# First modulation weights in tiles of 256 columns, first value products in halves of 256 features, router weights read later

## The chip, the cores and the metric

The kernel runs on one core of one Trainium2 chip. The metric is the device time of one execution in microseconds, given as the median of several runs. The profile comes from one more execution of the same program, recorded by the hardware profiler; its engines are named TensorE (PE, and PEld for its weight loads), VectorE (DVE), ScalarE (ACT), GpSimd (POOL) and SyncE (SP).

## The reference

Two layers of a diffusion backbone work on 256 latent tokens `x` and 256 context tokens `ctx` of 1024 features, all in float32. Only the start of layer 0 matters here:

```python
mod = jax.nn.silu(c) @ ada_w[layer] + ada_b[layer]
mod_c = jax.nn.silu(c_ctx) @ ada_w[layer] + ada_b[layer]
sh1, sc1, g1, sh2, sc2, g2 = [m[:, None, :] for m in jnp.split(mod, 6, axis=-1)]
...
xm = modulate(rmsnorm(h, norm_g[layer, 0]), sh1, sc1)      # x * (1 + sc1) + sh1
cm = modulate(rmsnorm(hc, norm_g[layer, 0]), sh1c, sc1c)
...
pl = xm @ w_in          # w_in: 1024 x 2560 = Fourier 256, q 768, k 768, v 768
pc = cm @ w_in
a_lat = fourier_mix(pl[..., :FNET_WIDTH])
```

After it come neighbourhood attention, an output projection, and a mixture of 16 experts whose router (`router_w`, `router_b`) picks two of them for a token. Layer 1 has retention with four decay matrices in place of the attention.

## The kernel before, in words

**Products in three parts.** A float32 product is done as three products of rounded float32: each operand is split into a high part (a rounded copy) and a low part (the rest). `mm3` (L318 to L320) issues high times high, low times high and high times low. For weights, `whi` is a copy on ScalarE (L176) and `wlo` a subtraction on VectorE or GpSimd (L178), both over 128x1024, so one tile of 1 MB has two of each.

**Weights.** All weights come in tiles of 1 MB on SyncE's queue, one after another in the order of the program, into a ring of four buffers called `raw` (L157). A load is issued when its buffer has been read for the last time; whatever stands behind it in the queue waits too. The first tiles are those of `ada_w`: 4 blocks of 128 rows by 512 columns, two tiles for a chunk of 512 of the 6144 modulation values. `ada_mm` (L259) loads a small bias `adab` (and for a scale the gain `adag`), multiplies the two columns of conditioning `cT` by the two tiles (L275), adds the bias on VectorE (L283, L285), turns the chunk by a TensorE transpose `ada_tp` (L289) and copies it to `modcol` (L290). Chunks 0 and 1 are the shift SH1, chunks 2 and 3 the scale SC1.

**The start of mixer0** (L354). `norm_t(t)` normalizes a block of 128 tokens (squares on ScalarE L218, a root on VectorE, the scaling `hn` L379), and sixteen transposes `nT` (L383) bring x's two blocks to features by tokens, copied by ScalarE into `mix` (L385). `modulate` (L388) takes a block of 128 features: scale and shift on VectorE (L397) or ScalarE (L395), the high part `xhi` on ScalarE (L399) and the low part `xlo` on VectorE (L400). The order is: x normalized, chunks 0 and 2, the first four blocks of x modulated, the first value weight tile split (one of its low parts on GpSimd), ctx loaded and normalized, its first four blocks modulated, chunks 1 and 3, and the last four blocks of both.

**Value products.** `v_ps` holds four PSUM tiles for the four blocks of tokens (two of x, two of ctx). The products over the first four feature blocks (kh 0) come first, for each token block t in turn, then those over the last four (kh 1), first for 512 columns of the values (n 0), then for the last 256 of them and the 256 Fourier columns (n 1), which ScalarE copies to `at` (L459).

**Decays and the Fourier part.** `decay_setup` makes four tables of decays (`d4`, one buffer) with eight exponentials each on ScalarE (L657, L660), masks and sums on VectorE (L661, L662), and a store of 512 KB from GpSimd's queue, `dmat` (L663). The exponentials of the next table that write into the buffer wait for the landing of the store before. Its inputs are read on ScalarE's queue (L621 the decay rates, L635 the distances `base`). The Fourier part multiplies `at` by a table (L465), copies the result to `ft` on ScalarE (L467), once for each of two halves b, and multiplies again (L472, L473). Then the query and key products `qk_ps` begin.

**The order of work.** Each engine and each queue executes its own list in order. A scheduler makes the lists of TensorE, ScalarE, VectorE and GpSimd from the program; `issue_after` adds a wish for one instruction to stand behind another. SyncE's list follows the program.

Of the kernel before, what the change touches and what calls it, by code (L numbers as in the profile page):

```python
# [7 lines left out]
F32 = mybir.dt.float32  # L8
# [4 lines left out]
ALU = mybir.AluOpType  # L13
# [8 lines left out]
SH1, SC1, G1, SH2, SC2, G2 = range(6)  # L22
C_ID, C_W4, C_PIDX, C_SEL, C_P = 0, 128, 132, 133, 149
C_U, C_IOTA = C_P, C_P + 128
# [53 lines left out]
def weight_tiles():  # L78
    t = {}
# [3 lines left out]
    t["ada_w"] = [((l,), 4 * i, 4, 512 * c, 512) for l in range(2) for c in range(12) for i in range(2)]  # L83
# [27 lines left out]
class Net:  # L111
# [110 lines left out]
    def prologue(self):  # L222
        nc, A = self.nc, self.A
# [13 lines left out]
        with self.tc.tile_pool(name="prop", bufs=1, space=PSUM, reuse_waits="tile") as p:  # L237
            tp = p.tile([128, 16], F32, name="ptp")
# [5 lines left out]
        nc.gpsimd.dma_start(self.rw, A["router_w"].rearrange("(k p) e -> p k e", p=128))  # L244
        self.rb = self.const.tile([128, 16], F32, name="rb")
        nc.gpsimd.dma_start(self.rb, A["router_b"].partition_broadcast(128))
        nc.gpsimd.tensor_scalar(self.rb, self.rb, 0.5, None, ALU.add)
# [4 lines left out]
        self.rbm = [self.const.tile([128, 16], F32, name=f"rbm{i}") for i in range(2)]  # L252

# [103 lines left out]
    def mixer0(self):  # L357
# [3 lines left out]
        with ExitStack() as es0:  # L361
# [5 lines left out]
            with ExitStack() as es:  # L367
# [5 lines left out]
                with ExitStack() as ea:  # L373
# [14 lines left out]
                    def modulate(k0, segs):  # L388
                        col = self.modcol[:, 0]
                        for k in range(k0, k0 + 4):  # L390
# [15 lines left out]
                    self.ada_chunk(0, 0, aps, psp)  # L406
                    self.ada_chunk(0, 2, aps, psp)
                    modulate(0, (0,))
                    self.prefetch_split([key(0, 4, 1792, 512)], 1)
                    nc.sync.dma_start(h[:, 2:4, :], A["ctx"].rearrange("(t p) d -> p t d", p=128))  # L410
                    norm_t(2)
                    norm_t(3)
# [7 lines left out]
                with ExitStack() as ea:  # L420
# [4 lines left out]
                    with tc.issue_after(ia.ins):  # L425
                        nc.scalar.dma_start(dft, A["cst"][:, C_BD:])
                        nc.scalar.dma_start(ui, A["cst"][:, C_U:C_U + 256])
# [8 lines left out]
                    for n in range(2):  # L436
# [5 lines left out]
                        for kh in range(2):  # L442
                            for t in range(4):
                                tk = slice(128 * t, 128 * t + 128)
                                with tc.issue_after(last.ins) if n + kh == 0 and t > 1 else ExitStack():
                                    for k in range(4 * kh, 4 * kh + 4):
                                        self.mm3(pss[t], (xhi[:, k, tk], xlo[:, k, tk]), self.wk(ws[kh], k % 4),
                                                 k == 0, k == 7)
                            if n:
                                self.ada_step(aps, psp)  # L450
# [1266 lines left out]
```

## Time and profile before

| | us |
|---|---|
| median of three runs (lowest, highest) | 1288.08 (1285.81, 1289.31) |
| the profiled execution's own time | 1290.84 |
| its span, from the first to the last instruction | 1289.0 |
| TensorE busy in the span | 1203.7 (93%) |
| VectorE busy | 941.8 (73%) |
| ScalarE busy | 755.6 (59%) |
| GpSimd busy | 124.5 (10%) |

A row of a timeline has the start, the busy time, the engine, the line, the operation, what is written from what, and the count of instructions in that row; the bracket tells how long the engine had been idle before it and what ended the idleness. A row of windows has the stretch and its length, then for each engine the busy time and the count, then the granted clock of TensorE as a share of its full 2.4 GHz, the mean busy share of the 16 DMA engines, and GB/s.

### The profile page before, as it was taken

What the parts mean: (1) busy time and instruction counts of PE and PEld (TensorE: products, weight loads), DVE (VectorE), ACT (ScalarE), POOL (GpSimd) and SP (SyncE); (2) the same over time, 40 slices, a digit from 0 to 9 for tenths busy, and PEclk for the clock granted to TensorE, in tenths of its full rate; (3) what the DMA queues carried; (4) which work ended last, traced back from release to release, by engine and by line L of the source; (5) the groups of instructions that cost most, each with busy time, mean ns of one, the idle gap of its engine ahead of it and who ended that gap; (6) DMA issues with size and microseconds to landing.
All of it is one profiled execution on the core that took longest, in us unless ns stands there. A gap on an engine that the chain in (4) does not pass through costs nothing. (4 is left out here: it accounts for less than half of the span.)

```text
span 1289.0 us, 18819 instructions
## 1 busy us (share of the span) xinstructions
PE 1203.7 (93%) x7093; PEld 946.8 (73%) x7093; DVE 941.8 (73%) x1601; ACT 755.6 (59%) x1122; POOL 124.5 (10%) x126
## 2 busy tenths in 40 slices
PE   4999999898699999999979999999997999999995
PEld 3777666566588888777668888898776788877673
DVE  4755666866698989888897554554657899888985
ACT  3753555723488888778544433343435777777663
POOL 1010102300111112111000000000004000000020
PEclk8999999999799999999989999999998999999998
DMA  9666774342899999999883445432749999889980
GB/s 348 254 238 244 270 256 153 106 166 102 332 354 373 365 363 365 359 362 347 299 326 111 147 157 199 154 119 98 270 174 359 369 369 367 336 334 344 336 335 9
DMA packets 60885, 340.60 MB, mean 264 GB/s; under 512 B 10252, under 2 KB 14860, under 8 KB 24144
## 3 DMA queue, kind: packets, MB, share of 16 engines
q1 hardware_dynamic: 46656, 303.07, 62.4%
q0 software_dynamic: 11392, 31.81, 7.6%
q10 hardware_dynamic: 2736, 4.41, 1.0%
q8 instruction: 59, 0.97, 0.3%
q14 instruction: 42, 0.34, 0.1%
HBM read 333.74 MB, written 18.40 MB: 273 GB/s over the span
## 5 line engine op out<-in xcount | busy, mean ns | idle before, releaser
L178 DVE TENSOR_TENSOR wlo<-raw,whi 128x1024 fp32r<-128x1024 f32 x471 | 558.8, 1221 | 114.2 <-ACT whi L176 113.0
L176 ACT ACTIVATE whi<-raw 128x1024 fp32r<-128x1024 f32 x476 | 481.2, 1054 | 106.8 <-PE qk_ps L319 24.5
L319 PE MATMUL h_ps<-wlo,xh 128*128 128x512 f32 x512 | 208.6, 407 | 4.5 <-DVE wlo L178 4.3
L318 PE MATMUL h_ps<-whi,xh 128*128 128x512 f32 x512 | 206.1, 403 | 3.3 <-ACT xh L1457 2.4
L320 PE MATMUL h_ps<-whi,xl 128*128 128x512 f32 x512 | 206.1, 402 | 0.1
L319 PEld LDWEIGHTS h_ps<-wlo,xh 128*128 128x128 f32 x512 | 97.6, 191 | 38.4 <-DVE wlo L178 17.6
L318 PEld LDWEIGHTS h_ps<-whi,xh 128*128 128x128 f32 x512 | 97.9, 191 | 26.0 <-ACT xh L1457 2.6
L320 PEld LDWEIGHTS h_ps<-whi,xl 128*128 128x128 f32 x512 | 97.6, 191 | 21.3 <-DVE xl L675 0.7
L275 PE MATMUL ada_ps<-raw,cT 128*32 128x128 f32 x1536 | 53.8, 276 | 2.1 <-DMA raw<-in_ada_w 2.1
L319 PE MATMUL y_ps<-wlo,gh 128*128 128x512 f32 (+1 forms) x136 | 53.5, 394 | 0.4 <-DVE wlo L178 0.3
L318 PE MATMUL y_ps<-whi,gh 128*128 128x512 f32 (+1 forms) x136 | 53.0, 391 | 0.7 <-ACT gh L674 0.7
L320 PE MATMUL y_ps<-whi,gl 128*128 128x512 f32 (+1 forms) x136 | 52.6, 395 | 0.1
L275 PEld LDWEIGHTS ada_ps<-raw,cT 128*32 128x32 f32 x1536 | 41.4, 110 | 13.9 <-issue 9.2
L319 PE MATMUL y<-wlo,gh 128*128 128x512 f32 x124 | 49.1, 396 | 0.4 <-DVE wlo L178 0.3
L318 PE MATMUL y<-whi,gh 128*128 128x512 f32 x124 | 49.2, 397 | 0.2 <-ACT gh L674 0.2
L320 PE MATMUL y<-whi,gl 128*128 128x512 f32 x124 | 48.4, 400 | 0.9 <-DVE gl L675 0.8
L1104 POOL DMA_INDIRECT moe_sum<-y,tok x15 | 28.1, 1877 | 158.1 <-ACT y L1099 158.1
L674 ACT ACTIVATE gh<-tsp 128x512 fp32r<-128x512 f32 x32 | 19.1, 596 | 41.4 <-PE tsp L671 41.2
L318 PE MATMUL qk_ps<-xhi,whi 128*128 128x512 f32 x96 | 39.4, 410 | 0.0
L319 PE MATMUL qk_ps<-xlo,whi 128*128 128x512 f32 x96 | 38.7, 403 | 0.0
L320 PE MATMUL qk_ps<-xhi,wlo 128*128 128x512 f32 x96 | 38.3, 399 | 0.0
L1604 POOL DMA_INDIRECT out_dram<-hg,tok x4 | 10.6, 2638 | 268.0 <-DVE hg L1598 218.4
(441 smaller groups left out, 2391.9 us busy)
## 6 DMA issues: line engine op xcount, KB each, us to landing
raw<-in_moe_w SPq DMA_DIRECT2D x188, 1024.0 KB, 7.6
raw<-in_ada_w SPq DMA_DIRECT2D x48, 1024.0 KB, 5.3
raw<-in_ret_w_in SPq DMA_DIRECT2D x24, 1024.0 KB, 5.7
raw<-in_mixab_w_in SPq DMA_DIRECT2D x10, 1024.0 KB, 5.6
raw<-in_ret_w_out SPq DMA_DIRECT2D x8, 1024.0 KB, 4.9
raw<-in_mixab_w_out SPq DMA_DIRECT2D x4, 1024.0 KB, 8.2
raw<-in_moe_w POOLq DMA_DIRECT2D x4, 1024.0 KB, 11.0
bias<-in_rpb ACTq DMA_DIRECT2D x12, 256.0 KB, 5.6
```

Of the source, the lines that this page charges most:

```text
L176: self.nc.scalar.activation(hi, r, AF.Copy)
L178: eng.tensor_tensor(lo, r, hi.bitcast(F32), ALU.subtract)
L275: mm = nc.tensor.matmul(ps[32 * j:32 * j + 32, 0:128], self.cT[:, kk, :], raw[:, k, 128 * j:128 * j + 128], start=(kk == 0), stop=(kk == 7 ...
L318: mm(out, lh, rh, start=first, stop=False)
L319: mm(out, lh, rl, start=False, stop=False)
L320: self.mm_last = mm(out, ll, rh, start=False, stop=last)
L674: i = nc.scalar.activation(hi[:, b0:b0 + w], tv, AF.Copy)
L1104: nc.gpsimd.indirect_dma_start(out=self.F[:, :], out_offset=bass.IndirectOffsetOnAxis(ap=R["tok"][:, e:e + 1], axis=0), in_=y, in_offset=N ...
L1604: self.nc.gpsimd.indirect_dma_start(out=self.out[:, :], out_offset=bass.IndirectOffsetOnAxis(ap=idx, axis=0), in_=x, in_offset=None, bound ...
```

## The change

Three things are written differently.

1. The four tiles of chunks 0 and 2 have 8 blocks of rows by 256 columns each, still 1 MB. A new `ada_half` does one half of a chunk with sixteen matmuls of half the height, with its own small tiles `adah` and `adahg` of 64 partitions (two buffers each). x's first four blocks are modulated two at a time; the first value weight tile is prepared between them, with all its low parts on VectorE; ctx is normalized behind the second pair.
2. The first products over the first four feature blocks are done, for the two token blocks of x, as two blocks for both and then the other two for both.
3. `router_w` and `router_b` are read on ScalarE's queue behind `ui` instead of on GpSimd's queue at the start.

```diff
-    t["ada_w"] = [((l,), 4 * i, 4, 512 * c, 512) for l in range(2) for c in range(12) for i in range(2)]
+    t["ada_w"] = [((0,), 0, 8, 512 * c + 256 * i, 256) for c in (0, 2) for i in range(2)]
+    t["ada_w"] += [((l,), 4 * i, 4, 512 * c, 512) for l in range(2) for c in range(12) for i in range(2)
+                   if l or c not in (0, 2)]
...
-        nc.gpsimd.dma_start(self.rw, A["router_w"].rearrange("(k p) e -> p k e", p=128))
-        nc.gpsimd.dma_start(self.rb, A["router_b"].partition_broadcast(128))
-        nc.gpsimd.tensor_scalar(self.rb, self.rb, 0.5, None, ALU.add)
...
+    def ada_half(self, vec, i, aps, psp, wp):
+        nc, A = self.nc, self.A
+        c, rs = 2 * vec, slice(64 * i, 64 * i + 64)
+        r = wp.tile([64, 128], F32, tag="adah", name="adah", bufs=2)
+        nc.sync.dma_start(r, A["ada_b"][0, c][rs])
+        if vec == SC1:
+            g = wp.tile([64, 128], F32, tag="adahg", name="adahg", bufs=2)
+            nc.sync.dma_start(g, A["norm_g"][0, 0, 0][rs])
+        raw = self.load(("ada_w", (0,), 0, 8, 512 * c + 256 * i, 256))
+        ps = aps[0].tile([128, 512], F32, tag=aps[1], name="ada_ps")
+        for k in range(8):
+            for j in range(2):
+                nc.tensor.matmul(ps[32 * j:32 * j + 32, 0:128], self.cT[:, k, :], raw[:, k, 128 * j:128 * j + 128],
+                                 start=(k == 0), stop=(k == 7), tile_position=(0, 32 * j))
+        nc.vector.tensor_tensor(r, ps[0:64, 0:128], r, ALU.add)
+        if vec == SC1:
+            nc.vector.scalar_tensor_tensor(r, r, 1.0, g, ALU.add, ALU.mult)
+        tp = psp.tile([128, 512], F32, tag="tp", name="ada_tp")
+        nc.tensor.transpose(tp[:, 0:64], r, self.ident[:64, :64])
...
-                    self.ada_chunk(0, 0, aps, psp)
-                    self.ada_chunk(0, 2, aps, psp)
-                    modulate(0, (0,))
-                    self.prefetch_split([key(0, 4, 1792, 512)], 1)
+                    for v in (SH1, SC1):
+                        self.ada_half(v, 0, aps, psp, wa)
+                    modulate(0, (0,), 2)
+                    self.prefetch_split([key(0, 4, 1792, 512)])
+                    for v in (SH1, SC1):
+                        self.ada_half(v, 1, aps, psp, wa)
+                    ia, iv = modulate(2, (0,), 2)
                     nc.sync.dma_start(h[:, 2:4, :], A["ctx"].rearrange("(t p) d -> p t d", p=128))
-                    norm_t(2)
-                    norm_t(3)
+                    with tc.issue_after(ia.ins), tc.issue_after(iv.ins):
+                        norm_t(2)
+                        norm_t(3)
...
-                        nc.scalar.dma_start(ui, A["cst"][:, C_U:C_U + 256])
+                        ui_dma = nc.scalar.dma_start(ui, A["cst"][:, C_U:C_U + 256])
+                    with tc.issue_after(ui_dma.ins):
+                        nc.scalar.dma_start(self.rw, A["router_w"].rearrange("(k p) e -> p k e", p=128))
+                        nc.scalar.dma_start(self.rb, A["router_b"].partition_broadcast(128))
+                    nc.gpsimd.tensor_scalar(self.rb, self.rb, 0.5, None, ALU.add)
...
-                            for t in range(4):
+                            ts = [(t, 4 * kh, 4) for t in range(4)]
+                            if n + kh == 0:
+                                ts[:2] = [(t, k, 2) for k in (0, 2) for t in range(2)]
+                            for t, k0, kn in ts:
```

The lists of the engines differ in places that the diff does not name. SyncE's queue at the start, before:

```order
L265 DMA adab<-in_ada_b 128x128
L157 DMA raw<-in_ada_w 128x2048 x2
L265 DMA adab<-in_ada_b 128x128
L268 DMA adag<-in_norm_g 128x128
L157 DMA raw<-in_ada_w 128x2048 x2
L157 DMA raw<-in_mixab_w_in 128x2048
L410 DMA h<-in_ctx 128x2x1024
```

and after:

```order
L257 DMA adah<-in_ada_b 64x128
L159 DMA raw<-in_ada_w 128x2048
L257 DMA adah<-in_ada_b 64x128
L260 DMA adahg<-in_norm_g 64x128
L159 DMA raw<-in_ada_w 128x2048
L159 DMA raw<-in_mixab_w_in 128x2048
L159 DMA raw<-in_ada_w 128x2048
L257 DMA adah<-in_ada_b 64x128 x2
L260 DMA adahg<-in_norm_g 64x128
L159 DMA raw<-in_ada_w 128x2048
L435 DMA h<-in_ctx 128x2x1024
```

The first value weight tile now stands ahead of the third modulation tile, and the fourth modulation tile stands behind a third and fourth `adah`, which have two buffers.

ScalarE's list around the third and fourth decay table (`d_701` and `d_723`, lines of `decay_setup`) and the Fourier copies (`at`, `ft`), before:

```order
L657 ACTIVATE e_724<-base,dbias,nl 128x256
L657 ACTIVATE e_728<-base,dbias,nl 128x256
L459 COPY at<-v_ps 128x256 x2
L176 ACTIVATE whi<-raw 128x1024
L459 COPY at<-v_ps 128x256
L657 ACTIVATE d_723<-base,dbias,dec_612 128x256 x2
L660 ACTIVATE d_723<-rel_637,dec_612 128x256
L660 ACTIVATE e_732<-rel_642,dec_612 128x256
L660 ACTIVATE d_723<-rel_647,dec_612 128x256
L660 ACTIVATE e_738<-rel_652,dec_612 128x256
L467 COPY ft_963<-f_ps 128x512
L467 COPY ft_964<-f_ps 128x512
```

and after, where the fourth table is `d_740`:

```order
L178 ACTIVATE whi<-raw 128x1024
L690 ACTIVATE e_741<-base,dbias,nl 128x256
L492 COPY at<-v_ps 128x256
L690 ACTIVATE e_745<-base,dbias,nl 128x256
L492 COPY at<-v_ps 128x256
L500 COPY ft_980<-f_ps 128x512
L690 ACTIVATE d_740<-base,dbias,dec_629 128x256 x2
L693 ACTIVATE d_740<-rel_654,dec_629 128x256
L693 ACTIVATE e_749<-rel_659,dec_629 128x256
L693 ACTIVATE d_740<-rel_664,dec_629 128x256
L693 ACTIVATE e_755<-rel_669,dec_629 128x256
L500 COPY ft_981<-f_ps 128x512
```

The exponentials of the fourth table stood ahead of both copies `ft`; they stand between them now.

VectorE's list over the sums of the third table, before:

```order
L662 TENSOR_TENSOR d_701<-d_701,e_706 128x256
L661 TENSOR_TENSOR d_701<-d_701,msk_638 128x256
L661 TENSOR_TENSOR d_701<-d_701,msk_648 128x256
L661 TENSOR_TENSOR e_710<-e_710,msk_643 128x256
L661 TENSOR_TENSOR e_716<-e_716,msk_653 128x256
L662 TENSOR_TENSOR d_701<-d_701,e_710 128x256
L662 TENSOR_TENSOR d_701<-d_701,e_716 128x256
L458 COPY vt<-v_ps 128x256 x2
L178 TENSOR_TENSOR wlo<-raw,whi 128x1024
```

and after, where the third table is `d_718`:

```order
L180 TENSOR_TENSOR wlo<-raw,whi 128x1024
L695 TENSOR_TENSOR d_718<-d_718,e_723 128x256
L694 TENSOR_TENSOR d_718<-d_718,msk_655 128x256
L694 TENSOR_TENSOR e_727<-e_727,msk_660 128x256
L694 TENSOR_TENSOR d_718<-d_718,msk_665 128x256
L695 TENSOR_TENSOR d_718<-d_718,e_727 128x256
L491 COPY vt<-v_ps 128x256
L694 TENSOR_TENSOR e_733<-e_733,msk_670 128x256
L180 TENSOR_TENSOR wlo<-raw,whi 128x1024
L695 TENSOR_TENSOR d_718<-d_718,e_733 128x256
```

Two low parts of weights that followed the sums stand among them now, the second ahead of the last sum, behind which the table is stored.

## Rows read from the trace of the kernel before

**Rows 1.** Windows of the span: stretch, busy time by engine, clock, DMA share, GB/s.

```profile
25.00:30.00 5.00, 4.46 (x10) 2.90 (x11) 3.65 (x14) 3.78 (x7) 2.50 (x1) 0.50 1.03 416
...
90.00:93.60 3.60, 3.48 (x8) 2.85 (x9) 3.57 (x10) 3.12 (x8) 1.08 (x2) 0.53 0.98 405
...
100.00:1289.00 1189.00, 1124.27 (x6408) 884.75 (x6406) 887.85 (x1442) 702.29 (x1025) 113.17 (x103) 0.98 0.71 263
```

**Rows 2.** Timeline of TensorE, 8 to 48 us.

```profile
14.64 2.14 PE L275 MATMUL ada_ps<-raw,cT 128*32 128x128 f32 x64
...
19.90 1.08 PE L275 MATMUL ada_ps<-raw,cT 128*32 128x128 f32 x32 [1.30 <-DMA raw<-in_ada_w]
...
25.50 1.22 PE L318 MATMUL v_ps<-whi,xhi 128*128 128x512 f32 x2 [3.31 <-ACT whi L176]
...
32.80 0.39 PE L320 MATMUL v_ps<-whi,xlo 128*128 128x512 f32 x1
33.03 1.03 PE L383 MATMUL nT<-cst,hn 128*128 128x128 f32 x8
...
47.64 0.73 PE L318 MATMUL v_ps<-whi,xhi 128*128 128x512 f32 x2 [0.82 <-ACT whi L176]
```

**Rows 3.** Timeline of ScalarE, 20 to 50 us.

```profile
22.50 0.60 ACT L395 ACTIVATE mix<-mix,modcol 128x256 f32<-128x256 f32 x1 [7.16 <-DVE modcol L290]
...
26.61 1.04 ACT L218 ACTIVATE hn<-h 128x1024 f32<-128x1024 f32 x1
```

**Rows 4.** Timeline of SyncE's queue: start of the issue, its length, what is loaded.

```profile
17.39 1.60 SPq L157 DMA_DIRECT2D raw<-in_ada_w  x2
...
88.22 3.02 SPq L157 DMA_DIRECT2D raw<-in_ada_w  x4
```

**Rows 5.** Timeline of VectorE, 16 to 46 us.

```profile
21.05 0.29 DVE L283 TENSOR_TENSOR adab<-ada_ps,adab 128x128 f32<-128x128 f32 x1 [3.25 <-PE ada_ps L275]
...
25.48 1.22 DVE L178 TENSOR_TENSOR wlo<-raw,whi 128x1024 fp32r<-128x1024 f32 x1 [0.95 <-ACT whi L176]
...
32.19 0.75 DVE L379 TENSOR_SCALAR hn<-h,rs_y 128x1024 f32<-128x1024 f32 x1
```

**Rows 6.** Timeline of GpSimd, 0 to 95 us.

```profile
26.79 2.50 POOL L178 TENSOR_TENSOR wlo<-raw,whi 128x1024 fp32r<-128x1024 f32 x1 [15.67 <-ACT whi L176]
...
86.69 0.57 POOL L663 DMA_DIRECT2D dmat<-d  x1 [11.10 <-DVE d L662]
```

**Rows 7.** Timeline of ScalarE again, 47 to 95 us, with its queue (ACTq).

```profile
47.85 0.81 ACTq L635 DMA_DIRECT2D base<-in_dist  x1
...
82.58 1.09 ACT L657 ACTIVATE d<-base,dbias,dec 128x256 f32<-128x256 f32 x2 [3.40 <-DMA dmat<-d]
...
89.96 1.09 ACT L657 ACTIVATE d<-base,dbias,dec 128x256 f32<-128x256 f32 x2
...
92.55 0.56 ACT L467 COPY ft<-f_ps 128x512 f32<-128x512 f32 x1
94.27 0.58 ACT L467 COPY ft<-f_ps 128x512 f32<-128x512 f32 x1 [1.15 <-PE f_ps L465]
```

**Rows 8.** Timeline of TensorE, 82 to 98 us.

```profile
88.45 1.13 PE L465 MATMUL f_ps<-dft,at 128*128 128x256 f32 x4 [2.40 <-ACT at L459]
90.12 4.11 PE L465 MATMUL f_ps<-dft,at 128*128 128x256 f32 x10 [0.54 <-ACT at L459]
...
97.19 0.50 PE L318 MATMUL qk_ps<-xhi,whi 128*128 128x512 f32 x1
```

**Rows 9.** DMA issues (KB each, median us to landing): whole span; then around 74, 86.7, 94.2 us.

```profile
raw<-in_ada_w SPq DMA_DIRECT2D x48, 1024.0 KB, 5.3
...
dmat<-d POOLq DMA_DIRECT2D x1, 512.0 KB, 8.7
...
dmat<-d POOLq DMA_DIRECT2D x1, 512.0 KB, 3.1
...
dmat<-d POOLq DMA_DIRECT2D x1, 512.0 KB, 8.2
```

More of the change, by code (lines that the diff above doesn't have):

```diff
@@ L252, in prologue @@
         self.rbm = [self.const.tile([128, 16], F32, name=f"rbm{i}") for i in range(2)]
+    def ada_half(self, vec, i, aps, psp, wp):
[17 more added lines that the diff above has]
+        nc.tensor.transpose(tp[:, 0:64], r, self.ident[:64, :64])
+        k0 = {SH1: 0, SC1: 8}[vec] + 2 * i
+        nc.vector.tensor_copy(self.modcol[:, 0, k0:k0 + 2, :],
+                              tp[:, 0:64].rearrange("p (j r) -> p j r", r=32)[:, :, 0:2])
     def ada_keys(self, layer, cs):
@@ L386, in norm_t, with modulate @@
                                            tp.rearrange("p (b q) -> p b q", q=128))
-                    def modulate(k0, segs):
+                    def modulate(k0, segs, n=4):
                         col = self.modcol[:, 0]
-                        for k in range(k0, k0 + 4):
+                        for k in range(k0, k0 + n):
                             for i in segs:
@@ L442, in mixer0 @@
                         for kh in range(2):
-                            for t in range(4):
+                            ts = [(t, 4 * kh, 4) for t in range(4)]
+                            if n + kh == 0:
+                                ts[:2] = [(t, k, 2) for k in (0, 2) for t in range(2)]
+                            for t, k0, kn in ts:
                                 tk = slice(128 * t, 128 * t + 128)
                                 with tc.issue_after(last.ins) if n + kh == 0 and t > 1 else ExitStack():
-                                    for k in range(4 * kh, 4 * kh + 4):
+                                    for k in range(k0, k0 + kn):
                                         self.mm3(pss[t], (xhi[:, k, tk], xlo[:, k, tk]), self.wk(ws[kh], k % 4),
```

## The prediction

> **What bounds the kernel now.** First I read the windows of the span [rows 1]. From 100 us to the end TensorE works 1124.27 us of 1189.00, so an early gain or loss of TensorE should stay in the total; the first 100 us, where the change acts, hold its larger holes. Then TensorE's timeline [rows 2]. It waits 1.30 us for the third modulation tile (the row at 19.90), then 3.31 us until the first value product at 25.50; the transposes of ctx follow at 33.03, and the products with the second half of the features start at 47.64. The weight tile's high part on ScalarE ends the 3.31 us wait, since modulation stands ahead of it there [rows 3]. A third look goes to the queues: what SyncE issues and when [rows 4]. Last come the decay tables and the Fourier part at 82 to 97 us [rows 6 to 9], because the order of both kernels differs there too though the diff says nothing of it.
>
> **The first value product.** It now needs half the modulation. TensorE's transposes of x end at 14.6 in either kernel. A chunk of 512 features costs 2.14 us for its first form [rows 2], a half 1.1. Both first half tiles are the first two loads on the queue, and TensorE began the first chunk, which needs the first two loads, at 14.64 without a wait for them [rows 2]; so the wait of 1.30 us, for a later tile, goes. Estimate: shift half 14.6 to 15.7, its add and transpose, scale half 16.2 to 17.3, and then what lies between add and first modulation: 21.05 to 22.50, 1.45 us [rows 3, 5]; on VectorE two low-part subtractions of 1.22 us [rows 5] now stand round the copy to `modcol`, because the one that took GpSimd 2.50 us [rows 6] is theirs as well. That gives a first product at about 21.4 instead of 25.5: **4 us earlier**. The second subtraction is no longer on GpSimd, which saves nothing more: TensorE met it late in the row of products.
>
> **What the lead meets.** The second scale half is the difficulty. Its tile stands on SyncE's queue behind two small bias loads whose two buffers are released only by TensorE's first two transposes of modulation, at about 18.1, so it is issued at about 19.6, where before everything up to the third chunk's tiles had gone out by 19.0 [rows 4]. One tile takes a median 5.3 us [rows 9]; 4.6 is my lower bound, so it lands at 24.2 to 24.9. By then the twelve products of the first half are through: at the granted clock of 0.50 one costs 0.45 us (ten in 4.46 us at 25 to 30 us [rows 1]), and at full clock 0.23 (32.80 to 33.03 [rows 2]); twelve end at 26.5 or at 24.4. Which of the two it is follows from the clock before: it was half from 25 to 30 us, behind a TensorE that had idled 3.3 us; in the changed kernel it still idles 2 us there, after work that is thinner. I take the half clock. Then: half chunk 1.1 us to 27.5, add to modulation 1.45, the modulation and split of two blocks about 1.4 (four blocks and two weight parts took 22.50 to 26.61, 4.1 [rows 3]; I take a third): ScalarE's squares of ctx, which the change puts behind these blocks, start at 30.4 instead of 26.61 [rows 3], **3.8 later**; at full clock, bounded by the tile, at 28.6, 2.0 later.
>
> Against that stands TensorE's work behind ctx. The squares lead to the last normalized row in 32.94 minus 26.61, 6.3 us [rows 3, 5], and its transposes at 33.03. From there to the second half's products before took 47.64 minus 33.03, 14.6 us. In that stretch lay the second batch of transposes, chunk products and six value products that the new order puts ahead of it; about 3 us of TensorE time leaves it (the six products 1.4, most of one chunk 1.6). So the second half starts 3.8 minus 3 later, **+0.9 us**; with full clock 2.0 minus 3, -1.1; with both batches at half clock +2.5. The lead of 4 us is thus gone before 50 us.
>
> **Router weights.** Two issues move to ScalarE's queue, ahead of the decay loads; one issue there took at most 0.81 us [rows 7]. The base table comes up to 1.6 later plus the transfer; what of that the weight parts hide, which ScalarE does at the same time, no row tells. I take **+0.3**, bounds 0 and +1.6, nearer to nothing because the Fourier copy below is late for another reason anyway. What they free at the start, a thin transfer beside x, is not on the path: x must be normalized and transposed before the first modulation, and TensorE was busy until the second tile had landed.
>
> **Decay tables and Fourier part.** Here the order moves. Call T the start of the third table's exponentials, 82.58 [rows 7], ended by the second table's landing. Before, the third table went out at 86.69, T+4.1, ahead of SyncE's four modulation loads at 88.22, T+5.6 [rows 4, 6]. It landed in 3.1 us; the second and the fourth, issued with 1 MB loads in flight, took 8.7 and 8.2 [rows 9]. Now VectorE has two low parts of 1.22 us [rows 5] and a copy between its sums of the third table, so the table goes out at T+6.8, while the low part that frees a buffer stands early: three loads go out by about T+3. The table so meets about 3 MB ahead of it, like those two. And the second Fourier copy, which before came behind the exponentials of the fourth table at 94.27 [rows 7] though those were through at 92.55, now stands behind exponentials that wait for the third table's landing. With a landing of 8.2, the exponentials starting at T+15.0 and lasting 2.6 (89.96 to 92.55 [rows 7]), the copy runs at T+17.7 where it was at T+11.7: 6 later. On TensorE the next products of that copy stand in line before all qk products, which started at 97.19 [rows 8]; about half of a modulation chunk, 0.5 to 1 us, has been put ahead of them as filler, so qk starts **5.5 later**. With a landing of 3.1 the copy is at T+12.6 and qk 0.9 later. Between lie 4 to 6 us landings. I take 8.2, because the table's situation is that of the rows with 8.2 and 8.7, with loads in front.
>
> A rule speaks against that value. The Trainium skill ("DMA: Bandwidth & Descriptors", section "Queues, rings and completion order") says that each DMA engine goes round between the queues that have work, packet by packet, so the table would not stand behind all of SyncE's 3 MB; that is rival E below. The trace does not agree well: 8.7 and 8.2 us with loads in flight, against 3.1 alone.
>
> The hole of some 5 us on TensorE can also lower its clock: before, TensorE idled 2.40 us up to 88.45, the granted clock was 0.53 from 90 to 93.6 us, and ten Fourier records from 90.12 took 4.11 us [rows 1, 8]; a second fall could cost 0 to 1.7.
>
> **Sum.** +0.9, +0.3 and +5.5 are +6.7 us on the profiled run of 1290.84, 1297.5. That run lies 2.8 above the median of 1288.08, against which times are taken: 1294.8, told as 1294.5. Slack behind 100 us that could swallow it isn't visible: of those 1189 us TensorE is idle in 65, spread over them.
>
> **Rivals.** (A) *The lead survives and the decays stay where they are.* The second scale tile must land by about 22, which needs SyncE's two small loads not to block, and the first products run at full clock. Then squares of ctx start no later than 26.6, the whole 4 us carries over, and the third table is issued ahead of the loads: 1288.1 - 4 = 1284. For it speaks that the transfers were full still at 25 to 30 us (share 1.03 [rows 1]), so that a short block of the queue may cost little; against it, the two buffers ahead of that tile. It decides if the squares of ctx begin before 26.6. (B) *The third table lands fast*, in about 3.1 us: +0.9 +0.3 +0.9 = +2.1, 1290. For it: the modulation loads may wait for their buffers longer than I think and go out behind the table. (E) *The table and the loads share the transfers equally*: the 3.1 us of the table alone doubles to 6.2 [rows 9], the copy runs at T+15.6, 4 later, qk 3.5: +0.9 +0.3 +3.5 = 4.7, 1292.8. For it: 0.5 MB on a queue of its own; against it the 8.2 and 8.7. (C) *Nothing arrives anywhere*: products start earlier, the second half starts when it did, and the Fourier copy hides its wait behind modulation products: 1288. That is the change not doing what it says. (D) *The half clock holds in both batches and falls again at the Fourier part*: +2.5 +0.5 +6 +1.7, about 1299.
>
> **Numbers.** The measurement can tell some 0.3%, 3.9 us, from no change: slower is above 1292.0, faster below 1284.2. Forecast 0.32, E 0.11, D 0.07: slower 0.50. B 0.24 and C 0.12: same 0.36. A and part-ways to it 0.14. The range takes in C, B, E, the forecast with its landing bounds and half of D, and leaves out A's own time and what is beyond D: 1285 to 1299. The likeliest case alone: 1292 to 1297.
>
> **What the profile after would show.** Right: first value product at 21 to 22 us; an idle stretch in the transfers at about 17 to 20; Squares of ctx at 28.5 to 30.5; second half at 47 to 49; the third table's landing at 7 to 9 us with SyncE's loads issued ahead of it; TensorE idle some 5 us before a Fourier product and ended by ScalarE's second copy; qk at 102 to 104. Wrong: a third table landing in about 3 us or issued ahead of the loads (then B); a modulation tile issued without waiting and Squares before 27 (then A); clock rows at 1.00 from 21 to 30 us (first term -1).

## The result and the profile after

The changed kernel takes 1300.01 us in the median (1295.58 to 1303.67, 4 runs), the kernel before 1288.15 (1285.81 to 1289.31, 4 runs). The ratio is 1.009 (95% interval 1.0066 to 1.0115): **slower by 12 us**. The profiled execution took 1295.58, the fastest of the four, with a span of 1293.8.

The start, on TensorE's timeline of the changed kernel (start, busy time, instruction, in the bracket the idle time before and what ended it):

```profile
22.44 0.50 PE L340 MATMUL v_ps<-whi,xhi 128*128 128x512 f32 x1 [0.91 <-ACT xhi L421]
...
26.66 1.94 PE L265 MATMUL ada_ps<-raw,cT 128*32 128x128 f32 x32 [0.77 <-DMA raw<-in_ada_w]
29.30 0.27 PE L271 MATMUL ada_tp<-cst,adah 64*128 64x64 f32 x1 [0.69 <-DVE adah L269]
30.76 0.69 PE L340 MATMUL v_ps<-whi,xhi 128*128 128x512 f32 x1 [1.19 <-ACT xhi L421]
...
36.30 1.09 PE L405 MATMUL nT<-cst,hn 128*128 128x128 f32 x8
...
49.11 1.20 PE L340 MATMUL v_ps<-whi,xhi 128*128 128x512 f32 x4 [0.82 <-ACT whi L178]
```

The first value product comes at 22.44, 3.1 us earlier than in [rows 2]. The fourth half chunk then waits for its tile, the transposes of ctx come at 36.30 instead of 33.03, and the second half starts at 49.11 instead of 47.64: the lead has become a delay of 1.5 us. A half chunk of modulation costs 1.94 us, nearly as much as a whole chunk of 512 columns did (2.14 in [rows 2]): it has half the matmuls (x32 records against x64), but they stand 0.061 us apart instead of 0.033. Each matmul has the size that it had (it is the half chunk that has half the height, not the matmul, as the section on the change puts it); what differs is that they go to two column strips of the array in turn, and before to four. So the two halves of a chunk, 3.88 us, cost 1.8 times the whole.

SyncE's queue shows why the tile is late (start of the issue, its length, what is loaded):

```profile
16.79 3.37 SPq L257 DMA_DIRECT2D adah<-in_ada_b  x2
20.21 0.59 SPq L260 DMA_DIRECT2D adahg<-in_norm_g  x1
20.85 1.19 SPq L159 DMA_DIRECT2D raw<-in_ada_w  x1
22.08 0.43 SPq L435 DMA_DIRECT2D h<-in_ctx  x1
```

The two small tiles hold the queue till 20.2; the modulation tile goes out at 20.85 and lands 5.7 us later. In the windows of the span the transfers are busy for 0.28 and 0.50 of the time meanwhile, where they had been full (1.01 in both stretches before), and TensorE keeps its full clock from 20 to 30 us (stretch, busy times of the five engines, clock, share of the DMA engines, GB/s):

```profile
15.00:20.00 5.00, 3.73 (x62) 3.11 (x58) 1.74 (x5) 1.73 (x2) 0.00 (x0) 1.00 0.28 111
20.00:25.00 5.00, 4.09 (x39) 3.12 (x35) 3.05 (x8) 1.44 (x3) 0.00 (x0) 1.00 0.50 159
25.00:30.00 5.00, 3.10 (x37) 2.21 (x35) 0.92 (x4) 0.19 (x1) 0.00 (x0) 1.00 1.01 413
30.00:35.00 5.00, 4.24 (x12) 3.34 (x12) 3.72 (x21) 3.10 (x7) 0.00 (x0) 0.66 1.02 410
...
95.00:100.00 5.00, 0.00 (x0) 0.00 (x0) 0.45 (x2) 1.14 (x3) 0.00 (x0) 0.92 0.85 351
100.00:105.00 5.00, 2.94 (x24) 2.04 (x28) 3.71 (x11) 2.78 (x9) 0.56 (x1) 0.50 0.22 84
```

Behind the wait for the fourth tile, from 30 to 35 us, the clock is down (0.66): the products of the second pair of blocks, from 30.76 on, stand 0.43 us apart instead of 0.23. The last two of these rows are the Fourier part: TensorE does nothing from 95 to 100 us, and runs at half clock from 100 to 105. Its timeline there, and then ScalarE's:

```profile
93.77 1.07 PE L297 MATMUL ada_ps<-raw,cT 128*32 128x128 f32 x30
102.06 1.23 PE L505 MATMUL f_ps<-ft,dft 128*128 128x258 f32 x2 [7.22 <-ACT ft L500]
103.08 1.05 PE L506 MATMUL f_ps<-ft,dft 128*128 128x254 f32 x2
104.07 2.20 PE L297 MATMUL ada_ps<-raw,cT 128*32 128x128 f32 x34
106.20 0.50 PE L340 MATMUL qk_ps<-xhi,whi 128*128 128x512 f32 x1
```

```profile
83.60 1.09 ACT L690 ACTIVATE d<-base,dbias,dec 128x256 f32<-128x256 f32 x2 [2.43 <-DMA dmat<-d]
...
91.29 0.58 ACT L500 COPY ft<-f_ps 128x512 f32<-128x512 f32 x1 [0.79 <-PE f_ps L498]
98.86 1.09 ACT L690 ACTIVATE d<-base,dbias,dec 128x256 f32<-128x256 f32 x2 [6.98 <-DMA dmat<-d]
...
101.45 0.57 ACT L500 COPY ft<-f_ps 128x512 f32<-128x512 f32 x1
```

The second copy `ft` stands behind exponentials that wait 6.98 us for the third table's store. GpSimd issued that store at 89.90, amid SyncE's four loads, and it took 8.9 us:

```profile
85.87 5.56 SPq L159 DMA_DIRECT2D raw<-in_ada_w  x4
```

```profile
89.90 0.57 POOL L696 DMA_DIRECT2D dmat<-d  x1 [10.46 <-DVE d L695]
```

```profile
dmat<-d POOLq DMA_DIRECT2D x1, 512.0 KB, 8.9
```

Three of the four loads were issued ahead of the store (4.0, 3.3 and 2.5 us before it), the fourth 1.2 us behind it. The first qk product comes at 106.20 instead of 97.19 [rows 8], **9.0 us later**. From there the two programs run alike, and the delay shrinks only by small steps: 7.8 us at the first attention output, 6.8 at the first products of the experts' second weights, 6.7 at the start of the second layer and 6.4 near its end, 4.9 from 1003 us. The last step is not a gain of the changed kernel: the profiled execution of the kernel before took 1.5 us more between 996 and 1003 us (7.55 from the last experts' table to the next products, against 6.05) than ten of the twelve other profiles of this study. Its clock was down there, as it was not in the changed kernel's (1.00):

```profile
998.00:1002.00 4.00, 3.77 (x10) 3.03 (x11) 2.37 (x6) 1.06 (x1) 2.95 (x3) 0.57 1.02 422
```

### The profile page after: what moved, and what is told of

Its sections match the earlier page's. It is cut to its first block, busy times and chain, and to the rows that moved or that the text cites. A ratio compares the mean times of both kernels' runs of the same rounds, so it can differ in the third digit from the quotient of the medians.

```text
span 1293.8 us, 18833 instructions
## 1 busy us (share of the span) xinstructions
PE 1202.8 (93%) x7095; PEld 947.2 (73%) x7095; DVE 942.7 (73%) x1607; ACT 755.7 (58%) x1122; POOL 122.2 (9%) x123
## 5 line engine op out<-in xcount | busy, mean ns | idle before, releaser
L297 PE MATMUL ada_ps<-raw,cT 128*32 128x128 f32 x1408 | 50.4, 279 | 0.0
L297 PEld LDWEIGHTS ada_ps<-raw,cT 128*32 128x32 f32 x1408 | 38.7, 111 | 11.6 <-issue 9.5
```

Of the source, the lines that this page charges most:

```text
L297: mm = nc.tensor.matmul(ps[32 * j:32 * j + 32, 0:128], self.cT[:, kk, :], raw[:, k, 128 * j:128 * j + 128], start=(kk == 0), stop=(kk == 7 ...
```

## The experiments

**Theory.** The loss sits at the Fourier part: the lists are ordered so that a copy for which TensorE waits stands behind a wait for a store that meets SyncE's loads. **Rival.** The halves at the start make it, by the late fourth tile. The experiments ran on three chips; each ratio below is taken against runs of the kernel before on the same chip.

**The router weights back at the start.** The other two parts of the change stay.

```diff
+        nc.gpsimd.dma_start(self.rw, A["router_w"].rearrange("(k p) e -> p k e", p=128))
+        nc.gpsimd.dma_start(self.rb, A["router_b"].partition_broadcast(128))
+        nc.gpsimd.tensor_scalar(self.rb, self.rb, 0.5, None, ALU.add)
...
-                    with tc.issue_after(ui_dma.ins):
-                        nc.scalar.dma_start(self.rw, A["router_w"].rearrange("(k p) e -> p k e", p=128))
-                        nc.scalar.dma_start(self.rb, A["router_b"].partition_broadcast(128))
-                    nc.gpsimd.tensor_scalar(self.rb, self.rb, 0.5, None, ALU.add)
```

> The changed kernel with its third part undone: router weights read on GpSimd's queue at the start again. In the lists of the engines this alone puts the exponentials of the fourth decay table back ahead of both Fourier copies on ScalarE. Theory 1 (the order of ScalarE's list around the Fourier copies makes the loss, and the halves cost little): TensorE's hole of 7.2 us before the last Fourier products goes, qk products start near 98 to 100 us instead of 106.2, and the time falls to about 1288 to 1292. Theory 2 (the halves at the start make the loss, through the late second scale tile): qk starts no earlier than about 104, and the time stays above 1295.

Measured: 1292.34 us against 1288.35 of before, ratio 1.0024 (1.001 to 1.0039). TensorE at the Fourier part, and the store's row, now issued at 88.75 ahead of SyncE's loads at 90.28:

```profile
95.24 0.70 PE L504 MATMUL f_ps<-ft,dft 128*128 128x258 f32 x2 [0.64 <-ACT ft L499]
...
98.39 0.51 PE L343 MATMUL qk_ps<-xhi,whi 128*128 128x512 f32 x1
```

```profile
dmat<-d POOLq DMA_DIRECT2D x1, 512.0 KB, 3.1
```

The hole of 7.2 us is gone and the store takes 3.1 us. What is left, 1.2 us at the qk products and 4 us in the medians, belongs to the first two parts of the change; the profile doesn't show where the rest of these 4 us lies. Theory 1 holds for two thirds of the loss (7.7 of 11.9 us).

**The router's move alone**, in the kernel before: the same lines the other way round.

> The kernel before with the third part of the change alone: router weights on ScalarE's queue behind ui. ScalarE's list then has the exponentials of the fourth table between the two Fourier copies, as in the changed kernel. Theory 1: a hole of 5 to 8 us before the last Fourier products and 1294 to 1299 us, though the start (first value product at 25.5 us, second half at 47.6) is as before. Theory 2: 1287 to 1290 us.

Measured: 1294.74 us, ratio 1.0045 (1.0031 to 1.0059). Its TensorE:

```profile
46.29 1.20 PE L315 MATMUL v_ps<-whi,xhi 128*128 128x512 f32 x4 [0.82 <-ACT whi L176]
...
101.13 1.23 PE L473 MATMUL f_ps<-ft,dft 128*128 128x258 f32 x2 [6.25 <-ACT ft L468]
...
105.41 0.51 PE L315 MATMUL qk_ps<-xhi,whi 128*128 128x512 f32 x1
```

The start is 1.35 us earlier than before (46.29 against 47.64), which was not expected: the wait of 1.30 us for a modulation tile [rows 2] is gone with the two loads at the start. And yet qk begins 8.2 us later, with the same hole. So two small loads that were moved to another queue turn the lists round, 40 us behind the place where they stand: this part alone is enough for the hole.

**Two buffers for the decay tables**, in the changed kernel:

```diff
-                d4 = s.tile([128, 4, 256], F32, tag="d4", name="d4")
+                d4 = s.tile([128, 4, 256], F32, tag="d4", name="d4", bufs=2)
```

> The changed kernel with two buffers for the decay tables instead of one, so that no exponential waits for the landing of the table just stored. Theory 1 (ScalarE waiting for the third table's landing is what TensorE pays for): the hole goes, qk starts at 96 to 100 us, and the time is 1285 to 1291. Theory 2: the hole is only moved to another wait (ScalarE's at copies, the clock), and the time stays above 1295.

Measured: 1291.3 us, ratio 1.0025 (1.0005 to 1.0045). TensorE has no wait any more from the first Fourier product to qk, at the full clock:

```profile
89.14 3.72 PE L498 MATMUL f_ps<-dft,at 128*128 128x256 f32 x16
...
95.82 0.50 PE L340 MATMUL qk_ps<-xhi,whi 128*128 128x512 f32 x1
```

qk starts 1.4 us earlier than in the kernel before, 10.4 us earlier than in the changed one, so the wait for the store is what TensorE paid for. Yet the time is 3 us above the kernel before, just outside what was expected: in the trace the lead turns into a delay later, 0.4 us at the output projection and 2.0 at the second layer's query products. The first of these steps is the clock, which was 1.00 in the same stretch of the kernel before:

```profile
243.00:246.00 3.00, 3.00 (x12) 1.23 (x8) 1.69 (x4) 1.15 (x5) 0.00 (x0) 0.59 0.00 0
```

What brings such a stretch isn't shown. It comes in some executions and not in others, so one profile of each kernel can't tell a difference of a microsecond at the end.

**Four small tiles instead of two**, in the changed kernel, so that SyncE isn't held:

```diff
-        r = wp.tile([64, 128], F32, tag="adah", name="adah", bufs=2)
+        r = wp.tile([64, 128], F32, tag="adah", name="adah", bufs=4)
...
-            g = wp.tile([64, 128], F32, tag="adahg", name="adahg", bufs=2)
+            g = wp.tile([64, 128], F32, tag="adahg", name="adahg", bufs=4)
```

> The changed kernel with four buffers instead of two for the small bias and gain tiles of the halves, so that SyncE issues the second scale half's tile without waiting for TensorE's transposes. ScalarE's list at the Fourier part stays as in the changed kernel. Theory: the tile lands 3 to 4 us earlier, the squares of ctx start at about 27.5 instead of 30.9, the second half of the value products at about 46 instead of 49.1. If the loss sits at the Fourier part and depends on the third table's landing alone, about 3 us of this reaches the end: 1295 to 1298. If the wait for the tile costs nothing (rival: TensorE's half clock in the first products replaces it), the second half starts at 48 to 49 and the time is 1298 to 1301.

Measured: 1296.6 us, ratio 1.0077 (1.0052 to 1.0102). SyncE's queue and TensorE:

```profile
16.58 0.33 SPq L159 DMA_DIRECT2D raw<-in_ada_w  x1
```

```profile
29.97 0.50 PE L340 MATMUL v_ps<-whi,xhi 128*128 128x512 f32 x1 [1.20 <-ACT xhi L421]
...
47.28 1.20 PE L340 MATMUL v_ps<-whi,xhi 128*128 128x512 f32 x4 [0.84 <-ACT whi L178]
```

The tile goes out 4.3 us earlier, at 16.58, which is when the ring of four weight tiles lets it go, and lands 4.9 us later. But the fourth half chunk, which now waits for nothing, starts at 25.86 instead of 26.66, since it stands behind ten products of the first pair in TensorE's list. So the squares of ctx start at 30.13 and not at the 27.5 expected, the second products of the first half at 29.97 instead of 30.76, the second half at 47.28 instead of 49.11, 1.8 us earlier and not the 3 expected: it is now where it was before the change. Of the 1.8 us, 0.8 are there when the second pair starts; the other 1.0 comes behind it, where the clock now stays up:

```profile
30.00:35.00 5.00, 4.98 (x52) 3.74 (x52) 4.10 (x24) 2.59 (x6) 0.00 (x0) 1.00 0.80 328
```

In all five traces of the halves with two small tiles it was down in this stretch (0.66 to 0.88), in all four with four it was 1.00. The time agrees with the theory, at the Fourier part the hole is there.

**The changed kernel again**, unchanged, for a second profile.

> The changed kernel once more, for a second profile and more times, since its four times spread from 1295.6 to 1303.7 and the one profile is that of the fastest. Theory 1 (the hole at the Fourier part is there in each run, about 9 us at the qk products, and later stages give back 1 to 4 us of it by where the routing of experts starts): qk products at 104 to 108 us again, median 1297 to 1300. Rival (the spread comes from the start, where the clock falls or not in the first value products): qk would lie at 110 or later, and the time with it.

Measured: 1303.65 us (1300.32 to 1308.36, 4 runs), ratio 1.0125 (1.0099 to 1.0151). The start is like the first profile's, the second half at 49.32. qk comes at 108.01, 1.8 us later than in the first one, and the attention 2.7 later. The windows of the two executions, the first one's two rows ahead of the second one's, tell the difference:

```profile
90.00:95.00 5.00, 4.29 (x44) 3.38 (x44) 1.28 (x2) 1.09 (x3) 1.60 (x3) 1.00 1.01 388
...
105.00:110.00 5.00, 5.00 (x38) 4.00 (x31) 0.69 (x3) 0.00 (x0) 1.13 (x2) 0.90 0.94 321
```

```profile
90.00:95.00 5.00, 3.65 (x11) 2.69 (x12) 2.77 (x5) 2.13 (x5) 1.70 (x3) 0.78 1.02 385
...
105.00:110.00 5.00, 5.00 (x41) 3.45 (x41) 1.10 (x4) 0.44 (x2) 1.39 (x3) 0.52 0.78 272
```

In the second execution the clock was down already at 90 to 95 us, so that ten Fourier records took 3.95 us instead of 2.42, was up again for part of the hole, and was down to 110. So these two executions differ where the kernel idles, not at their start. The median lies above the 1297 to 1300 expected. The start varies as well, though. In the run with two buffers above, whose instructions are the same up to there, the first half chunk took 2.94 us instead of 1.94 and the second half started at 50.92; in the run with the router's loads behind the distance table, below, the figures are 2.95 and 50.46. The row of the former:

```profile
14.67 2.94 PE L265 MATMUL ada_ps<-raw,cT 128*32 128x128 f32 x32
```

**Both repairs**: two buffers for the tables and four small tiles, in the changed kernel.

> The changed kernel with both repairs: four buffers for the small tiles of the halves, and two buffers for the decay tables. Theory: the second half of the value products starts at about 47.3, as with four buffers alone, no exponential waits for a store, qk starts at 92 to 94 us, three to five earlier than in the kernel before, and the time is 1283 to 1287. Rival (what is gained at the start is given back behind the attention, as in the run with two buffers alone, which lost 1.7 us there and 1.2 more at 690 us): 1287 to 1291.

Measured: 1287.96 us, ratio 0.9989 (0.9972 to 1.0006): as fast as before, the rival's figure. Part of it is what the rival said: a lead of 1.2 us at qk turns into a delay of 0.5 in the attention, where the clock is down for a while:

```profile
200.00:203.00 3.00, 3.00 (x13) 2.70 (x14) 2.00 (x8) 1.50 (x5) 0.00 (x0) 0.54 1.03 416
```

But qk itself comes at 96.0, not at the 92 to 94 expected. The second half starts at 47.85, but the Fourier products only at 89.33, 4 us later than in the kernel before. TensorE has one wait in between, for a weight's low part on VectorE, whose list has that low part behind the decay inputs, which wait for the distance table:

```profile
63.16 0.50 PE L341 MATMUL v_ps<-wlo,xhi 128*128 128x512 f32 x1 [1.93 <-DVE wlo L180]
```

```profile
57.59 0.49 DVE L681 TENSOR_SCALAR rel<-base 128x256 f32<-128x256 f32 x2 [3.79 <-DMA base<-in_dist]
```

and TensorE's clock is down around it (0.87 and 0.79 from 60 to 70 us). That table's load was issued at 49.67, behind the two router loads (46.71 and 47.90); before it was used at 53.51. But with four small tiles alone the same loads go out in the same order, the table's at 48.90, and VectorE uses it at 53.13 without a wait. So this wait is that of one execution; it is not shown that the router's move brings it.

**Two buffers for the decay tables in the kernel before**, and nothing else.

> The kernel before with two buffers for the decay tables and nothing else. Theory: ScalarE's copies of the Fourier columns no longer stand behind exponentials that wait for a store, the idle 2.40 and 0.54 us of TensorE before the Fourier products go and with them the half clock there; qk starts at 93 to 95 us instead of 97.2, and the time is 1284 to 1287. Rival (the gain is given back later): 1287 to 1290.

Measured: 1283.05 us (1281.38 to 1284.98), ratio 0.9955 (0.9938 to 0.9973). **Faster than both kernels**, and a little faster than expected.

```profile
85.12 3.72 PE L465 MATMUL f_ps<-dft,at 128*128 128x256 f32 x16
...
91.80 0.50 PE L318 MATMUL qk_ps<-xhi,whi 128*128 128x512 f32 x1
```

The sixteen Fourier records follow one another at the full clock; before they took 0.70, 1.13 and 4.11 with waits of 2.40 and 0.54 [rows 8]. qk starts 5.4 us earlier, and the lead stays to the end. On another chip, beside the next two, the same kernel gave 1285.47 us, ratio 0.9978 (0.996 to 0.9995):

> The kernel before with two buffers for the decay tables, once more, beside the run of the halves with the same two buffers: 1282 to 1285 again, qk products at about 91.8 us. If the gain of 5 us were a matter of the chip or the hour, it would come out at 1286 or more.

That is just above what was expected, with qk at 92.07 again: the lead in the trace repeats, its size in the times less well.

**The halves with four small tiles, without the router's move.**

> The changed kernel without the router's move and with four buffers for the small tiles: the halves at their best with the order of ScalarE as in the kernel before. Theory (the halves are worth nothing even when no small tile blocks SyncE, since the ring of four weight tiles holds the second scale tile until TensorE has read the first): the second half starts at 47 to 48.5, qk at 96.5 to 98, time 1286 to 1290. Rival (a lead of 2 us or more reaches the end): qk at 95 or before, below 1286.

Measured: 1290.39 us, ratio 1.0013 (0.9999 to 1.0028). The second half starts at 47.05, 0.6 us before the kernel before, and qk at 96.26, 0.9 before. The halves at their best, with one buffer for the tables, gain nothing in the time.

**The same with two buffers for the tables**, which leaves the router's move as the difference to the run with both repairs.

> Halves with four small tiles and two buffers for the decay tables, router weights at the start as in the kernel before. Against the run with all three parts (1288.0) it tells what the router's move costs when no exponential waits for a store; against the kernel before with two buffers (1283.1) what the halves are worth. Theory 1: the router's move still costs 2 to 4 us, since the distance table comes later behind it and VectorE's list has a weight low part behind that table (TensorE waited 1.9 us for it at 63 us): 1284 to 1286, no wait of TensorE between 48 and 90 us. Theory 2: that wait comes with the halves: 1287 to 1290. In either the halves are worth nothing (second half at 47 to 48 us as before): not below 1282.

Measured: 1284.38 us, ratio 0.9968 (0.9952 to 0.9984). There is no wait of TensorE between 48 and 85 us, and qk starts at 93.24:

```profile
93.24 0.50 PE L343 MATMUL qk_ps<-xhi,whi 128*128 128x512 f32 x1
```

The run with both repairs, which has the router's move besides, is 3.6 us slower in the median and 2.8 at qk. That isn't shown to be the price of the move. The two ran on two chips, between which the kernel before with two buffers differs by 2.4 us, and the ratios (0.9968 and 0.9989) have intervals that overlap. And the 2.8 us at qk are the wait at 63 us and the clock behind it, which the other traces with the move don't have: from the start of the second half to the first Fourier product it takes 37.7 us in the kernel before, 37.7 to 38.7 in six traces with the move (one of them with four small tiles, one with two buffers), and 41.5 only in the run with both repairs. Against the kernel before with two buffers, beside which it ran, the halves are worth nothing that can be told: 1284.38 and 1285.47.

**The router's loads behind the distance table**, in the changed kernel:

```diff
             nc.scalar.dma_start(base, A["dist"])
+            with self.tc.issue_after(base_dma.ins):
+                nc.scalar.dma_start(self.rw, A["router_w"].rearrange("(k p) e -> p k e", p=128))
+                nc.scalar.dma_start(self.rb, A["router_b"].partition_broadcast(128))
```

> The changed kernel with the router's loads on ScalarE's queue behind the distance table instead of ahead of the decay rates and that table. ScalarE's list still has the exponentials of the fourth table between the two Fourier copies. Theory 1 (the list's order costs most): the first use of the distance table comes 2 us earlier, but the hole before the last Fourier products is 5 to 8 us again and the time 1296 to 1302. Rival (the two loads ahead of the distance table cost most): 1288 to 1293.

Measured: 1299.22 us, ratio 1.0081 (1.0055 to 1.0107), as slow as the changed kernel. The distance table's first use comes 5.3 us behind the start of the second half (55.74 and 50.46), against 8.1 in the changed kernel (57.17 and 49.11), but the hole is there:

```profile
102.78 1.23 PE L501 MATMUL f_ps<-ft,dft 128*128 128x258 f32 x2 [7.25 <-ACT ft L496]
```

So the two loads ahead of the distance table aren't what costs most; the order of ScalarE's list is.

## Why the prediction was right and wrong

The sign, the place and the mechanism were right; the range (1285 to 1299) missed the median by 1.0 us, and the forecast of 1294.5 lay 5.5 too low. By its steps:

- *First value product 4 us earlier, about 21.4.* It came at 22.44, 3.1 earlier. A half chunk was priced at 1.1 us from 2.14 for a chunk; it took 1.94. The 32 records of half a chunk took 1.08 in the kernel before [rows 2], in four strips; in two strips they take 0.9 more, and all four half chunks lie on the path to the squares of ctx. (The tile that the row at 19.90 waits for is the fourth modulation tile, not the third; nothing hangs on it.)
- *The fourth tile issued at 19.6, landing at 24.2 to 24.9.* It was issued at 20.85 and landed 5.7 us later, 26.6. That the two small tiles block the queue was right. The clock was put down in the wrong batch: the first pair of blocks ran at 1.00 from 20 to 30 us, behind a wait of 0.91 us where it had been 3.31, and the second pair, behind the wait for the tile, at 0.66 from 30 to 35, nine products 0.43 us apart instead of 0.23. The errors cancel: ctx's squares started at 30.93 (30.4 was forecast), the second half at 49.11, +1.5 instead of +0.9. That this term came out near is luck; by the prediction's own sign for the clock it should have been -1. (Its twelve products from 21.4 on end at 26.8 or 24.2 by its own prices, not at 26.5 or 24.4, which changes little.)
- *Router weights +0.3.* TensorE lost 0.5 us between 49 and 87 us in the changed kernel, half of it in a wait for a low part, within the bounds. The bound of 1.6 was counted from 0.81 us as the longest issue on that queue; the one before it, of `ui`, took 1.33 and the second router load's 1.44, so the distance table was issued 1.8 us later, counted from the start of the second half. In one of the other traces TensorE lost 3.8 us in this stretch (both repairs), in the rest 0.9 or less. That what the loads free at the start is not on the path was wrong in the kernel before, where the move alone brought the second half 1.35 us forward; with the halves it brought nothing (47.28 with the move and 47.05 without, four small tiles in both). What the prediction hadn't seen is that this part alone also turns ScalarE's list round; it took the new order as given.
- *The third table.* Issue at T+6.8, landing 8.2, copy at T+17.7. Measured with T = 83.60: issue at T+6.3, landing 8.9, copy at T+17.85. The rows with loads in flight (8.7 and 8.2) were the right ones to take, and the row alone (3.1) is what the store takes when it goes out ahead of the loads, in the run without the router's move. Rival E, equal turns at 6.2 us, is not what happened: 8.9 to 9.1 in all five traces with three loads ahead. By the Trainium skill's rule ("DMA: Bandwidth & Descriptors", "Queues, rings and completion order") a store on another queue gets its turn packet by packet; here it took nearly three times its time alone.
- *qk 5.5 us later.* **This is the term that failed, by its size.** The copy itself came when it was forecast to come: 7.2 us later than before (101.45 against 94.27), where the sum had 0.9 and 0.3 for the shift and 6 for the copy. What followed the copy was wrong. The clock behind the hole had been priced at 0 to 1.7 and taken at 0, and half a us was even taken off for modulation products put into the hole. In both profiles the clock was at half after the hole. From the copy's end to the first qk product it took 4.2 us instead of 2.3 (102.02 to 106.20 against 94.85 to 97.19), though 30 modulation records had gone into the hole. So qk came 9.0 us later where the sum had 6.7; 7.5 of the 9.0 were lost behind the start of the second half, where the sum had 5.8. In the second execution the clock was down ahead of the hole too (0.78 from 90 to 95 us) and still after qk had begun (0.52 from 105 to 110): 10.5 us at the attention.
- *The sum on the profiled run, less 2.8 to the median.* This step failed too. That the profile of the kernel before lay above its median was right to take off: 1.5 us of it are those at 996 to 1003 us, where its clock was down. But the two profiles of the changed kernel are of its fastest runs (1295.58 of a median of 1300.01, 1300.32 of 1303.65). The two profiled runs differ by 4.7 us, less than the 6.7 forecast, and the medians by 11.9. At the first attention output the traces show 7.8 and 10.5 us, the medians 12 and 15. Where the other 4 to 5 us lie in the runs that have no trace isn't settled. The clock would fit in the first group, not in the second: over the runs of the kernel before, on each of three chips, a mean granted clock lower by 0.001 goes with 0.65 to 0.67 us more (an estimate from a straight line through 21 to 24 runs), and the first profiled execution had 0.979 where the median of its four is 0.975, 2.7 of 4.4 us; the second had 0.973, as its group's median has.

Rival A didn't happen. With four small tiles its conditions came true, the tile landing at 21.5 and the first products at full clock, and the squares of ctx still began at 30.13: the fourth half chunk stands behind products of the first pair in TensorE's list, and it costs 1.94 us. Rival B is what happens when the order is undone.

## What to carry to other kernels

When a scheduler lays out the lists, compare the lists over the whole stage, not only at the lines changed: here two loads of 72 KB together, moved to another queue, put a copy that TensorE needed behind a wait for a store, and cost more than the rest of the change brought. A single buffer that is refilled after a store made ScalarE, and through it TensorE, wait here for that store's landing; a second buffer (4 KB on each partition) removed 5.4 us on one chip and 2.8 on another, in the kernel before, where nobody had meant to change anything at that place. A lead at the start is worth what the last of its inputs allows; ask which queue, place in the engine's list and clock each of them meets before counting it. And where one profile of each kernel is compared, look at the granted clock over the whole span first: here a stretch at half clock that came in one execution and not in the other moved the end by 1 to 2 us.

## What the runs showed of the hardware

- A store of 512 KB on GpSimd's queue took 2.9 to 3.1 us where the loads issued ahead of it on SyncE's queue had landed, or did within 0.3 us. It took 7.5 to 9.3 us behind two loads of 1 MB issued 1.1 to 2.5 us before it (six traces), 8.2 to 9.1 behind three or four issued 2.0 to 6.0 before (eight traces), and 5.3 to 7.1 behind two of which the first was issued 3.0 to 6.0 before (nine traces). In all 28 places where a load issued ahead was still under way and the traces have both landings, the store landed behind the last of these loads, by 0.3 to 2.8 us, and none of 17 loads issued while it was under way landed before it. So it came in the order of issue, though it stood on another queue.
- Modulation matmuls of 32 by 128 outputs took 0.033 us each when issued to four column strips in turn (2.14 us for 64 records) and 0.061 in two strips (1.94 for 32). That the strips work at the same time would explain it; no run took that apart. The first half chunk of a kernel took up to 2.95 us in other executions.
- After 7.2 us without work TensorE's granted clock was 0.50 for the next 5 us; products of 258 columns took 1.23 us for two, against 0.60 to 0.68 at full clock, and a modulation chunk's half 2.20 against about 1.1. After waits of 2.0 to 2.4 and 0.5 us ahead of the Fourier products the clock fell in two executions (4.11 and 3.96 us for ten records) and not in a third (2.42, with the router weights back at the start).
